# Moving the contents of twelve matmul operand buffers by 4 to 56 elements within their SBUF rows, in a four-layer decoder trunk in float32

## The chip, the cores and the metric

One core of one Trainium2 chip runs the whole program in a single launch. The metric is the device time of one execution in microseconds (us); the kernel before was run three times, and the median is used. "ns" is nanoseconds.

## The reference, cut to what matters

The input x has 512 tokens of 1024 channels. Four blocks follow one another, each added to the residual x: an even mixer (attention with forget gates beside a pooling mixer), a gated MLP, a Conformer convolution module, and a second gated MLP. Nearly all of the arithmetic is in products of a float32 weight matrix with the normed residual or with a hidden array:

```python
def even_mixer(h, ...):                     # h: (512, 1024)
    z = h @ w_in                            # 1024 -> 2056: q, k, v, forget logits, u
    a_out = forgetting_attention(q, k, v, f_logit, q_g, k_g)
    p_out = multiscale_pool(u, w_pool, pool_scale)
    return concat([a_out, p_out]) @ w_out   # 1024 -> 1024
def conformer_conv(h, ...):
    a, g = split(h @ w_pw1, 2)              # 1024 -> 2048
    u = causal_dwconv(a * sigmoid(g), dw_w, dw_b)     # 31 taps
    return silu(layer_norm(u, ln_g, ln_b)) @ w_pw2    # 1024 -> 1024
def conv_ffn(h, ...):                       # twice
    u = causal_dwconv(h @ w_up, conv_w, conv_b)       # 1024 -> 5632, 3 taps
    gate, val = split(u, 2)
    return (silu(gate) * val) @ w_down      # 2816 -> 1024
```

## The kernel before

**Layout.** Channels lie on the 128 partitions and tokens along a partition's row, so an array of 1024 channels is a tile of 8 slices (k = 0 to 7) of 128 x 512. A block of weights is 128 x 1024 (8 slices of 128 x 128), and one block gives one 128-channel slice of an output.

**Three products for one.** Each operand is kept as two tiles of the matmul type `fp32r`: a high part (`wh`, `xh`, `ah`, `mh`, `zh`) and the rest (`wl`, `xl`, `al`, `ml`, `zl`). `products` (L155) issues for every slice three matmuls with 512 columns: stationary `wh` against the moving high part (L159), stationary `wh` against the moving low part (L160), stationary `wl` against the moving high part (L161). One block of weights against 8 slices is therefore 24 matmuls. TensorE loads the stationary operand of a matmul while the one before it runs.

**Weights.** A block comes by DMA from SyncE's queue into `raw` (`load_raw`, L132). ScalarE copies it to `wh` (`w_high`, L137; the copy is L139) and VectorE, or GpSimd in part of the attention, subtracts to make `wl` (`w_low`, L142; L144). Each of the three has three buffers, under one tag `wr`, `wh`, `wl` of the pool `wp`.

**Moving operands.** `Normed` (L189) holds the residual times the norm's weight as `xh` and `xl`, 8 slices each, in one place for the whole kernel. The attention and pooling outputs go to `mh` and `ml` (L341, L342); the MLP's hidden array goes to `ah` and `al`, 22 slices each (L894, L895); the Conformer's to `zh` and `zl`.

**Stages in order.** The attention stage multiplies `xh`/`xl` by 3 + 2 + 8 weight blocks (keys, queries, gate, pooling input), forms the values with `xh`/`xl` as the stationary side, and runs the softmaxes between the products; TensorE's order there is written by hand, and VectorE's and ScalarE's order there is found by a scheduler. Then the output projection (`mh`/`ml`, 8 blocks), the first MLP (up: 44 blocks against `xh`/`xl`; down: 8 outputs of 22 slices against `ah`/`al`), the Conformer stage (16 blocks against `xh`/`xl`, with the taps on VectorE, GpSimd, ScalarE and TensorE in an order that a planner sets, then 8 blocks against `zh`/`zl`), and the second MLP.

**Where the tiles lie.** SBUF addresses are bytes within a partition's row. The program places `xh` at 36,768 and `xl` at 53,152, `wh` at 85,920, 90,016 and 94,112, `wl` at 98,208, 102,304 and 106,400: all seven and more leave 160 modulo 256. `zh` and `zl` also leave 160. `ah` (114,720) and `al` (159,776) leave 32, `mh` (135,392) and `ml` (151,776) leave 224. Slices are 2048 bytes apart in the moving tiles and 512 bytes apart in the weights, so every slice of a tile has its tile's residue.

Of the kernel before, what the change touches and what calls it, by code (L numbers as in the profile page):

```python
# [16 lines left out]
P = 128  # L17
# [18 lines left out]
# Columns of the parameter array, one value per partition and column.  # L36
# [11 lines left out]


class Plan:  # L50
    """Tasks, each on one engine, that are issued in the order of a simulated run: of the tasks
    that can start first, the one with the lowest key does. A task may take slots (of a pool's
    tag, say) that others give back. Costs and lags are in microseconds."""
# [43 lines left out]
def hybrid_trunk(ctx: ExitStack, tc: tile.TileContext, x, prm, w_qk, w_v, w_f, w_u, w_pool,  # L97
# [9 lines left out]
    # PSUM: 8 banks, by use in the attention; the other phases take them in turn  # L107
# [29 lines left out]
    def w_high(raw, shape):  # L137
        wh = wp.tile([P, *shape], F32R, tag="wh", name="wh", bufs=3)
        S.activation(out=wh, in_=raw, func=AF.Copy)  # L139
        return wh  # L140

    def w_low(raw, wh, shape, on=V):  # L142
        wl = wp.tile([P, *shape], F32R, tag="wl", name="wl", bufs=3)
        on.tensor_tensor(out=wl, in0=raw, in1=wh.bitcast(F32), op=ALU.subtract)  # L144
        return wl
# [5 lines left out]
    def load(src, shape, on=V):  # L151
        """A block of weights, and its parts: h + l is the block exactly."""
        return load_parts(load_raw(src, shape), shape, on)

    def products(acc, terms, first=True, last=True):  # L155
        """acc += sum of a.T @ b over (ah, al, bh, bl), each operand in two parts."""
# [6 lines left out]
    def split(src, h, l, g=None):  # L163
        """h + l = src, or src * g with one g per partition."""
# [8 lines left out]
    # A row of T values that all partitions of a 32-partition block hold is folded to T / 32  # L173
    # columns (value 32 j + p at partition p of the block, column j) and unfolded.
# [14 lines left out]
    class Normed:  # L189
        """The residual's parts times the norm's weight, and 1 / rms of every token, which  # L190
        the products are multiplied by afterwards."""

        def __init__(self, gname, goff, tmp):
            self.g, self.goff, self.tmp = gname, goff, tmp
            self.h = per.tile([P, KT, T], F32R, tag="xh", name="xh")
            self.l = per.tile([P, KT, T], F32R, tag="xl", name="xl")
# [31 lines left out]
    def even_layer(next_norm):  # L228
        with tc.tile_pool(name="att", bufs=1) as at, tc.tile_pool(name="att2", bufs=2) as a2, \
                tc.tile_pool(name="att4", bufs=4) as a4:  # L230
            # the first tiles of x and of the weights together, so that the products start early
# [27 lines left out]
            # eps * mean square, for the norms of q and k; 1 / rms with tokens on partitions  # L259
# [25 lines left out]
            # The logits of a head: [qh; qh].T @ [kh; kl] + [ql; row sums].T @ [kh; columns],  # L285
            # where the rows past q and k give c[q] - c[k]. Head 0 of a pair has them below,
            # head 1 above.
# [3 lines left out]
            # log forget gates, their running sum: at partitions 0-31 and 64-95, four times each  # L291
# [32 lines left out]
            # values, tokens on partitions  # L324
            # (where x was: it is loaded again for the residual)
# [15 lines left out]
            mh = at.tile([P, KT, T], F32R, name="mh")  # L341
            ml = at.tile([P, KT, T], F32R, name="ml")  # L342
# [11 lines left out]
            def qk_finish(pr, acc_k, acc_q, m_k, m_q):  # L354
                """The RMS norms of q and k, on products that are not multiplied by 1 / rms
                of x: that only weighs eps. Then the operands of the logits."""
# [70 lines left out]
            # What TensorE does while the softmaxes run: the next pairs' projections, the pooling,  # L427
            # the first outputs' products.
# [8 lines left out]
            def fill():  # L437
# [3 lines left out]
                later = [(1, finish1)]          # (steps to go, what then, a part every step)  # L441
# [577 lines left out]
```

## Time and profile before

| what | value |
|---|---|
| three runs | 1133.15, 1135.85, 1138.61 us (median 1135.85) |
| span of the profiled execution | 1134.6 us |
| its own time beside the median | 1.3 us below it |
| instructions in its trace | 12,732 |
| TensorE matmuls in the trace | 4,876, busy 1093.5 us (96% of the span) |
| VectorE / ScalarE / GpSimd busy | 749.2 / 508.0 / 152.3 us |
| read from HBM | 107.18 MB, 98 GB/s with what is written |

The profile is of one execution. "PE" is TensorE's matmuls and "PEld" its loads of the stationary operand, "DVE" is VectorE, "ACT" ScalarE, "POOL" GpSimd. A matmul's recorded duration reaches past the start of the next one, since matmuls are pipelined, so the cost of a matmul in a dense run is the time from one start to the next, called its spacing below. "L159" is line 159 of the kernel before. A granted clock of 1.00 is TensorE's upper level, 2.4 GHz, and 0.50 its lower one, 1.2 GHz.

### The profile page before, as it was taken

What the parts mean: (1) busy time and instruction counts of PE and PEld (TensorE: products, weight loads), DVE (VectorE), ACT (ScalarE), POOL (GpSimd) and SP (SyncE); (2) the same over time, 40 slices, a digit from 0 to 9 for tenths busy, and PEclk for the clock granted to TensorE, in tenths of its full rate; (3) what the DMA queues carried; (4) which work ended last, traced back from release to release, by engine and by line L of the source; (5) the groups of instructions that cost most, each with busy time, mean ns of one, the idle gap of its engine ahead of it and who ended that gap; (6) DMA issues with size and microseconds to landing.
All of it is one profiled execution on the core that took longest, in us unless ns stands there. A gap on an engine that the chain in (4) does not pass through costs nothing.

```text
span 1134.6 us, 12732 instructions
## 1 busy us (share of the span) xinstructions
PE 1093.5 (96%) x4876; PEld 872.2 (77%) x4876; DVE 749.2 (66%) x1049; ACT 508.0 (45%) x707; POOL 152.3 (13%) x131
## 2 busy tenths in 40 slices
PE   7999989999999999999999997799999999999998
PEld 5778867888888888888877762588888888888886
DVE  5888985677777776333359998777777777752221
ACT  6577644444444444222247544555444444431120
POOL 0031350000000000000039886000000000000000
PEclk9999999999999999999999998899999999999999
DMA  6211024223322233232324535132322232223330
GB/s 229 80 59 38 24 77 167 94 93 101 104 93 93 94 105 94 84 101 85 107 98 134 161 93 142 56 124 98 94 93 93 97 108 93 93 84 120 105 118 19
DMA packets 36972, 111.94 MB, mean 99 GB/s; under 512 B 4144, under 2 KB 4784, under 8 KB 36912
## 3 DMA queue, kind: packets, MB, share of 16 engines
q1 hardware_dynamic: 36912, 111.14, 31.2%
q8 instruction: 38, 0.62, 0.2%
q14 instruction: 22, 0.18, 0.0%
HBM read 107.18 MB, written 3.94 MB: 98 GB/s over the span
## 4 chain that ended last, share of the span: by engine, by line
PE 81%; DVE 8%; ACT 4%; POOL 3%; issue 1%; DMA 1%; POOLq 0%; SPq 0%; ACTq 0%; DVEq 0%
PE bank L161 26%; PE bank L159 26%; PE bank L160 26%; POOL y L733 2%; DVE bank L749 1%; ACT tap L730 1%; ACT wh L139 1%; PE bank L703 1%; DVE u L675 1%; DVE wl L144 1%; PE bank L873 1%; PE bank L874 1%; DMA raw<-in_w_qk 1%; DVE nm L500 1%; DVE pl L167 0%
## 5 line engine op out<-in xcount | busy, mean ns | idle before, releaser
L159 PE MATMUL bank<-xh,wh 128*128 128x512 f32 x936 | 371.3, 397 | 7.0 <-ACT wh L139 6.7
L160 PE MATMUL bank<-xl,wh 128*128 128x512 f32 x936 | 367.7, 393 | 0.0
L161 PE MATMUL bank<-xh,wl 128*128 128x512 f32 x936 | 367.3, 392 | 0.0
L139 ACT ACTIVATE wh<-raw 128x1024 fp32r<-128x1024 f32 (+2 forms) x189 | 193.4, 1026 | 288.3 <-PE bank L160 244.5
L144 DVE TENSOR_TENSOR wl<-raw,wh 128x1024 fp32r<-128x1024 f32 (+2 forms) x178 | 216.6, 1219 | 152.5 <-ACT wh L139 150.5
L159 PEld LDWEIGHTS bank<-xh,wh 128*128 128x128 f32 x936 | 177.3, 190 | 47.3 <-ACT wh L139 7.6
L161 PEld LDWEIGHTS bank<-xh,wl 128*128 128x128 f32 x936 | 177.1, 189 | 38.6 <-DVE wl L144 0.8
L160 PEld LDWEIGHTS bank<-xl,wh 128*128 128x128 f32 x936 | 177.4, 190 | 38.0 <-issue 1.4
L161 PE MATMUL bank<-ah,wl 128*128 128x512 f32 x352 | 139.0, 395 | 0.0
L159 PE MATMUL bank<-ah,wh 128*128 128x512 f32 x352 | 139.0, 395 | 0.0
L160 PE MATMUL bank<-al,wh 128*128 128x512 f32 x352 | 139.0, 395 | 0.0
L910 DVE SCALAR_TENSOR_TENSOR y<-u,pt,y 128x511 f32<-128x511 f32 (+1 forms) x176 | 131.7, 748 | 7.7 <-ACT y L907 4.6
L905 DVE TENSOR_TENSOR u<-bank,rstd 128x512 f32<-128x512 f32 x88 | 60.6, 688 | 79.0 <-PE bank L161 79.0
L733 POOL TENSOR_TENSOR y<-y,tap 128x512 f32<-128x512 f32 x54 | 81.4, 1508 | 10.0 <-ACT tap L730 6.5
L166 ACT ACTIVATE ah<-y 128x512 fp32r<-128x512 f32 x44 | 27.8, 632 | 114.9 <-DVE y L915 114.9
L161 PEld LDWEIGHTS bank<-ah,wl 128*128 128x128 f32 x352 | 66.1, 188 | 16.1
L160 PEld LDWEIGHTS bank<-al,wh 128*128 128x128 f32 x352 | 66.1, 188 | 16.1
L159 PEld LDWEIGHTS bank<-ah,wh 128*128 128x128 f32 x352 | 66.1, 188 | 16.0
L907 ACT ACTIVATE y<-u,pt 128x512 f32<-128x512 f32 x88 | 71.4, 811 | 4.8 <-DVE u L905 3.8
L914 ACT ACTIVATE y<-y 128x512 f32<-128x512 f32 x44 | 27.9, 634 | 83.0 <-DVE y L910 83.0
L219 DVE TENSOR_TENSOR xr<-bank,xr 128x512 f32<-128x512 f32 x32 | 22.0, 691 | 64.0 <-PE bank L161 64.0
L749 DVE SCALAR_TENSOR_TENSOR bank<-u,pt,bank 128x512 f32<-128x512 f32 x79 | 56.7, 747 | 0.7
(190 smaller groups left out, 1050.4 us busy)
## 6 DMA issues: line engine op xcount, KB each, us to landing
raw<-in_w_up SPq DMA_DIRECT2D x88, 512.0 KB, 3.3
raw<-in_w_down SPq DMA_DIRECT2D x32, 512.0 KB, 3.5
raw<-in_w_pw SPq DMA_DIRECT2D x24, 512.0 KB, 3.3
stack<-d SPq DMA_DIRECT2D x28, 256.0 KB, 5.1
raw<-in_w_down SPq DMA_DIRECT2D x16, 384.0 KB, 3.2
xr<-in_x SPq DMA_DIRECT2D x16, 256.0 KB, 6.0
raw<-in_w_qk SPq DMA_DIRECT2D x8, 512.0 KB, 3.3
raw<-in_w_out SPq DMA_DIRECT2D x8, 512.0 KB, 3.3
```

The lines of the kernel that those rows point to most:

```text
L139: S.activation(out=wh, in_=raw, func=AF.Copy)
L144: on.tensor_tensor(out=wl, in0=raw, in1=wh.bitcast(F32), op=ALU.subtract)
L159: PE.matmul(acc, lhsT=ah, rhs=bh, start=(first and i == 0), stop=False)
L160: PE.matmul(acc, lhsT=ah, rhs=bl, start=False, stop=False)
L161: PE.matmul(acc, lhsT=al, rhs=bh, start=False, stop=(last and i == n - 1))
L166: S.activation(out=h, in_=src, func=AF.Copy)
L733: G.tensor_tensor(out=mine["y2"], in0=mine["y2"], in1=mine[s], op=ALU.add)
L749: V.scalar_tensor_tensor(out=acc, in0=shifted(s), scalar=wcol(s), in1=acc, op0=ALU.mult, op1=ALU.add)
L905: V.tensor_tensor(out=u, in0=acc, in1=nrm.r, op=ALU.mult)
L907: S.activation(out=y, in_=u, func=AF.Identity, scale=col("cv_w", 3 * ct + 2), bias=col("cv_b", ct))
L910: V.scalar_tensor_tensor(out=y[:, s:], in0=u[:, 0:T - s], scalar=col("cv_w", 3 * ct + 2 - s), in1=y[:, s:], op0=ALU.mult, op1=ALU.add)
L914: S.activation(out=ys[0], in_=ys[0], func=AF.Silu)
```

## The change

Twelve buffers (three `wh`, three `wl`, and `xh`, `xl`, `ah`, `al`, `mh`, `ml`) are allocated 64 elements longer, and what they hold begins some elements into them. The rotation over three weight buffers, which the pool did under one tag, is now written as three tags taken in turn. No instruction is added or removed on any engine's list of work. Comments are also gone from the file; they are left out here.

```diff
+OFFSETS = {"wh0": 24, "wh1": 28, "wh2": 32, "wl0": 24, "wl1": 28, "wl2": 32,
+           "xh": 24, "xl": 36, "ah": 16, "al": 28, "mh": 56, "ml": 4}
...
+    turns = {"wh": itertools.cycle(range(3)), "wl": itertools.cycle(range(3))}
+
+    def placed(pool, shape, tag, name):
+        n = math.prod(shape)
+        t = pool.tile([P, max(n, 1024) + 64], F32R, tag=tag, name=name, bufs=1)
+        o = OFFSETS[tag]
+        t = t[:, o:o + n]
+        if len(shape) == 1:
+            return t
+        names = "abc"[:len(shape)]
+        return t.rearrange(f"p ({' '.join(names)}) -> p {' '.join(names)}",
+                           **dict(zip(names, shape)))
...
     def w_high(raw, shape):
-        wh = wp.tile([P, *shape], F32R, tag="wh", name="wh", bufs=3)
+        wh = placed(wp, shape, f"wh{next(turns['wh'])}", "wh")
...
     def w_low(raw, wh, shape, on=V):
-        wl = wp.tile([P, *shape], F32R, tag="wl", name="wl", bufs=3)
+        wl = placed(wp, shape, f"wl{next(turns['wl'])}", "wl")
...
-            self.h = per.tile([P, KT, T], F32R, tag="xh", name="xh")
-            self.l = per.tile([P, KT, T], F32R, tag="xl", name="xl")
+            self.h = placed(per, [KT, T], "xh", "xh")
+            self.l = placed(per, [KT, T], "xl", "xl")
...
-            mh = at.tile([P, KT, T], F32R, name="mh")
-            ml = at.tile([P, KT, T], F32R, name="ml")
+            mh = placed(at, [KT, T], "mh", "mh")
+            ml = placed(at, [KT, T], "ml", "ml")
...
-            ah = fp.tile([P, FT, T], F32R, name="ah")
-            al = fp.tile([P, FT, T], F32R, name="al")
+            ah = placed(fp, [FT, T], "ah", "ah")
+            al = placed(fp, [FT, T], "al", "al")
```

An element has 4 bytes. With the allocations that the changed program gets, the contents leave these residues modulo 256 (before in brackets): first weight buffer 0, second 16, third 32, the same for `wh` and `wl` (160); `xh` 0 and `xl` 48 (160); `ah` 96 and `al` 144 (32); `mh` 192 and `ml` 240 (224). `zh`, `zl` and all other tiles keep theirs.

The scheduler, which sees other buffers, also puts some instructions of VectorE and ScalarE in another order between the end of the attention and the start of the output projection; on GpSimd and SyncE the order is the same, and TensorE's differs only in how the three matmuls of neighbouring slices of the output projection follow one another. Here is VectorE's queue before, at the last pooling group: `us` are GpSimd's running sums, `mx` what VectorE makes of them, `nm` and `z` a softmax's row maximum and row sum, `p` its weights, `ml` the low part of a pooling output.

```order
L504 RECIPROCAL z<-z 128x1
L505 TENSOR_SCALAR p<-p,z 128x512
L504 RECIPROCAL z<-z 128x1
L505 TENSOR_SCALAR p<-p,z 128x384
L144 TENSOR_TENSOR wl<-raw,wh 128x128
L170 SCALAR_TENSOR_TENSOR ml<-bank,pt,mh 128x512
L500 TENSOR_REDUCE nm<-bank 128x1
L406 SCALAR_TENSOR_TENSOR mx<-us,u 128x512
L504 RECIPROCAL z<-z 128x1
L408 TENSOR_TENSOR mx<-us,pt 128x15
L505 TENSOR_SCALAR p<-p,z 128x256
```

And the same place in the changed program, where line numbers are 17 higher (L423 was L406, L522 was L505):

```order
L521 RECIPROCAL z<-z 128x1
L522 TENSOR_SCALAR p<-p,z 128x512
L517 TENSOR_REDUCE nm<-bank 128x1
L184 TENSOR_TENSOR pl<-bank,ph 128x128
L423 SCALAR_TENSOR_TENSOR mx<-us,u 128x512
L521 RECIPROCAL z<-z 128x1
L161 TENSOR_TENSOR wl<-raw,wh 128x128
L522 TENSOR_SCALAR p<-p,z 128x384
L187 SCALAR_TENSOR_TENSOR ml<-bank,pt,mh 128x512
L517 TENSOR_REDUCE nm<-bank 128x1
L425 TENSOR_TENSOR mx<-us,pt 128x15
L427 TENSOR_TENSOR mx<-mx,u 128x15
```

The instruction that reads GpSimd's `us` now stands ahead of the scaling of the softmax's 384-column block, the small `wl`, the `ml` and a row maximum, which it followed before.

## Rows read from the trace of the kernel before

**Rows 1.** The profile's page: busy time by engine, and TensorE's clock in 40 slices.
```profile
PE 1093.5 (96%) x4876; PEld 872.2 (77%) x4876; DVE 749.2 (66%) x1049; ACT 508.0 (45%) x707; POOL 152.3 (13%) x131
...
PEclk9999999999999999999999998899999999999999
```

**Rows 2.** The page: the chain that ended last, by engine.
```profile
PE 81%; DVE 8%; ACT 4%; POOL 3%; issue 1%; DMA 1%; POOLq 0%; SPq 0%; ACTq 0%; DVEq 0%
```

**Rows 3.** Waits: who, for whom, us in total, times, longest.
```profile
ACT wh L139 <- PE bank L160: 244.5, 142, 4.8
...
PE bank L159 <- ACT wh L139: 7.0, 2, 6.7
```

**Rows 4.** Windows: stretch, its us; each engine's busy us (instructions); clock, DMA, GB/s.
```profile
240.00:420.00 180.00, 180.00 (x796) 149.05 (x795) 131.71 (x166) 81.88 (x100) 0.00 (x0) 1.00 0.29 97
785.00:985.00 200.00, 200.00 (x884) 165.62 (x883) 146.62 (x185) 90.58 (x112) 0.00 (x0) 1.00 0.30 97
1010.00:1125.00 115.00, 115.00 (x495) 92.51 (x494) 30.28 (x31) 21.40 (x22) 0.00 (x0) 1.00 0.31 95
187.00:212.00 25.00, 25.00 (x111) 20.52 (x110) 18.24 (x24) 11.90 (x17) 0.00 (x0) 1.00 0.42 136
626.90:629.20 2.30, 2.30 (x7) 1.81 (x6) 1.94 (x4) 1.87 (x3) 2.14 (x3) 0.50 1.05 230
600.00:700.00 100.00, 89.51 (x440) 61.71 (x442) 95.99 (x120) 52.15 (x77) 88.97 (x66) 0.94 0.52 133
```

**Rows 5.** Groups of TensorE's instructions by shape: count, busy us, mean ns, idle before.
```profile
L159 PE MATMUL bank<-xh,wh 128*128 128x512 f32 x936 | 371.3, 397 | 7.0 <-ACT wh L139 6.7 <-ACT xh L169 0.3
...
L159 PE MATMUL bank<-ah,wh 128*128 128x512 f32 x352 | 139.0, 395 | 0.0
```

**Rows 6.** Timeline of TensorE in the first MLP's down projection: start us, us, what.
```profile
520.13 0.39 PE L159 MATMUL bank<-ah,wh 128*128 128x512 f32 x1
520.36 0.40 PE L160 MATMUL bank<-al,wh 128*128 128x512 f32 x1
520.60 0.39 PE L161 MATMUL bank<-ah,wl 128*128 128x512 f32 x1
```

**Rows 7.** Timeline of TensorE, 512-column weighted sums of the attention, second head.
```profile
95.44 0.39 PE L160 MATMUL bank<-pl,vhl 128*128 128x512 f32 x1
95.66 0.40 PE L161 MATMUL bank<-ph,vhl 128*128 128x512 f32 x1
95.90 0.34 PE L159 MATMUL bank<-ph,vhl 128*128 128x384 f32 x1
```

**Rows 8.** Timeline of TensorE at the lower clock, Conformer stage.
```profile
626.81 0.63 PE L159 MATMUL bank<-xh,wh 128*128 128x512 f32 x1
...
628.94 0.63 PE L161 MATMUL bank<-xh,wl 128*128 128x512 f32 x1
```

**Rows 9.** Timeline of TensorE after an idle stretch, values stage: first and tenth of a run.
```profile
28.89 0.39 PE L160 MATMUL bank<-wl,xh 128*128 128x512 f32 x1
...
30.97 0.39 PE L160 MATMUL bank<-wl,xh 128*128 128x512 f32 x1
```

**Rows 10.** Timeline of VectorE at the last pooling group; brackets: idle before, releaser.
```profile
160.62 1.00 DVE L505 TENSOR_SCALAR p<-p,z 128x384 f32<-128x384 f32 x1
...
163.26 0.41 DVE L500 TENSOR_REDUCE nm<-bank 128x1 f32<-128x256 f32 x1
165.09 0.69 DVE L406 SCALAR_TENSOR_TENSOR mx<-us,u 128x512 f32<-128x512 f32 x1 [1.42 <-POOL us L401]
```

**Rows 11.** Timeline of TensorE there: three blocks of transposes, and the last weighted sum.
```profile
166.34 0.51 PE L513 MATMUL bank<-ident,p 128*128 128x128 f32 x3
...
168.78 0.38 PE L513 MATMUL bank<-ident,p 128*128 128x128 f32 x2
...
170.39 0.27 PE L513 MATMUL bank<-ident,p 128*128 128x128 f32 x1
...
171.03 0.49 PE L159 MATMUL bank<-ph,vhl 128*128 128x512 f32 x1 [0.37 <-ACT ph L166]
```

## The prediction

> **What bounds the kernel now.** I read the page first. TensorE is busy 96% of the span and at the upper clock in all but a few slices [rows 1], and it holds 81% of the chain that ended last [rows 2]. The list of waits says the same from the other side: ScalarE waits 244.5 us in 142 places for TensorE to give back a `wh` buffer, while TensorE waits 7.0 us for ScalarE's copies [rows 3]. So in the MLPs and the projections weights are ready early, and a matmul's spacing is what counts. The exception is the Conformer stage: between 600 and 700 us VectorE is busy for 95.99 of 100 us [rows 4], so the 16 x 24 = 384 matmuls against `xh`/`xl` there can grow or shrink behind it.
>
> Next I worked out spacings. A window of dense matmuls counts those that hang over its edges, 1.7 of them (a record of 0.39 us over a spacing of 0.23). In the up projections that gives 180 / (796 - 1.7) and 200 / (884 - 1.7), both 226.7 ns; in the second down projection 115 / (495 - 1.7) = 233.1 ns; in the output projection 25 / (111 - 1.7) = 228.7 ns [rows 4]. All have 512 columns, the same types, the same clock of 1.00. At the lower clock, five spacings of the same form take 2.13 us, 426 ns each [rows 4, 8]; that is 512 columns at 1.2 GHz, one per cycle and nothing more. Half of it, 213 ns, would be the same at 2.4 GHz. **So 13 to 20 ns of each spacing at the upper clock are something else.**
>
> What differs between the stages is where the tiles lie. Call d the moving tile's residue less that of the stationary tile being loaded meanwhile, modulo 256. The up projections have d = 0, the output projection 224 - 160 = 64, the down projection 32 - 160, that is 128. The attention's weighted sums, 96 - 160, have 192: two spacings take 0.46 us, 230 ns each, read to 0.01 us [rows 7]. VectorE's load does not explain it: it is busy 73% of the time in the up projection, 26% in the slower down projection [rows 4].
>
> **The change part by part.** It adds no instruction. The three tags in turn repeat what one tag with three buffers did; I cost that at nothing, since the weights' side has the 244.5 us of slack above [rows 3], and a late `wh` would show first there. ScalarE and VectorE now write at 16-byte offsets; the traces show no such row, and the same slack covers it in the projections.
>
> *Spacing.* The new d differ by weight buffer (residues 0, 16, 32) and by tile. I interpolate linearly between the rows, with 226.7 at 0, 228.7 at 64, 233.1 at 128, and 232 at 192 (between the 230 just read and the 233 at 128). Nothing in this trace lies between the multiples of 64, so this is an estimate.
> - `xh` then has d = 0, 240, 224: mean 228.0, +1.3 ns. `xl` has 48, 32, 16: 227.7, +1.0. Two of three spacings move `xh`, so +1.2. The page of groups has 936 x 3 = 2808 of these [rows 5]; less the Conformer's 384 that is 2424, **+2.9 us**.
> - `ah` has 96, 80, 64: 229.8, -3.3 ns; `al` has 144, 128, 112: 232.6, -0.5. Mean -2.4, times 352 x 3 = 1056 [rows 5]: **-2.5 us**.
> - The output projection's 8 x 24 = 192: `mh` 192, 176, 160 gives 232.3, `ml` 229.3, mean +2.6: **+0.5 us**.
> - The Conformer's second product, 192 more: `zh` and `zl` stay, the weights move, so d = 160, 144, 128 in place of 0: 232.8, +6.1 ns, **+1.2 us**.
> - The 96 matmuls of the values stage, +0.1 us.
>
> Together +2.2 us. Taking the trace's rows as the ends, every spacing of the first and fourth item at 226.7 or at 233.1 would give -2 to +17 us; the floor of 213 ns lies far below, and I keep it for a rival. I take +2.2, since these d lie closest to the rows used.
>
> The Trainium skill's page "TensorE: Matmul & The Clock Gate" (section "Back-to-back issue gap") gives N / 2.4 + 2.5 ns, 215.8 ns for 512 columns, at the upper clock. By it the spacing that could be won is 11 to 17 ns and not 13 to 20; the trace shows no dense float32 run at that value.
>
> *Order.* At the last pooling group VectorE waited 1.42 us for GpSimd's `us` and began `mx` at 165.09 us [rows 10]. Before that wait it had done the scaling of the 384-column block (160.62, 1.00 us) and the row maximum of the next block (163.26) [rows 10]. In the changed order both stand behind the wait, with a small `wl` and the `ml`. So the scaled block comes at about 165.1 + 0.7 + 1 + 1 = 167.8 instead of 161.6, and TensorE, which transposes it at 166.34 [rows 11], stands there some 1.5 us. The row maximum moves from 163.3 to 168.5; exponential, scaling and two more blocks follow it, so the last transposes, at 170.39 [rows 11], come about 3 us later, and the weighted sum at 171.03, which waited 0.37 us already, with them. Another block's `wl` ahead of the last pooling `ml` adds a little, and one fewer wait after it gives some back. I take **+3.3 us**, with ends 0 (fill work slides into the gap) and +5 (all of 160 to 165 lost). What is late next is the end of the attention, and all after it.
>
> Sum: 1134.6 + 2.2 + 3.3 = 1140.1 for the profiled execution. It lay 1.3 us under the median of the three runs, so **1141.4 us**, 0.5% above 1135.85. A measurement of this kernel can tell about 0.5%, 5.7 us, from no change; the forecast stands on that edge.
>
> **The rivals.**
> *The residues free the moving stream (faster).* What costs 13 to 20 ns is the load of the next weights taking reads from the moving operand, and some pairs of residues keep them apart. For: the cost is there only at the upper clock, and differs by d [rows 4, 8]. Against: d = 0, which the change mostly leaves or surrounds, is the cheapest of four values seen. If half the way to 213 ns were won, about 2712 matmuls now at 226.7 would give 6.7 ns each (18 us), 1056 would give 10 (10.5 us) and 192 would give 8 (1.5 us): 30 less, 3.3 for the order, 1109 us; all the way, 1079. It decides from 2.3 ns per matmul on: 3960 of them then pay for the order and for 5.7 us.
> *The steady run is lost (slower).* In the up projection every spacing is 226.7. After an idle stretch it is not: the first nine take 2.08 us, 231.1 each [rows 9], and the down projection's run long and short in turn, 0.23 and 0.24 us [rows 6]. So the phase between the two streams matters, and equal residues let it settle at the best. With three weight buffers and two tiles at different residues it might never settle: 2712 x 4.4 = 11.9 us more, the down projections 2.1 less, +0.5 for the rest, +3.3: 1149.5 us. At 238, the largest spacing that a down row allows, it would be above 1165.
> *Residues do nothing, only the order counts.* The spacing would follow from something else that differs by stage, and 1139 us (1136 without the order) comes out. Against it: same shape, same clock, same engine, 6.4 ns apart [rows 4]. The Trainium skill's page "SBUF — State Buffer" (section "Who interferes with whom") speaks for this rival and against the change: TensorE has two independent read ports, one for each operand, and never waits on anyone. By that rule the residue term is zero and 1139 is the time; the trace disagrees in so far as it has the 6.4 ns.
>
> **How the numbers follow.** The forecast has 0.42 (its own range 1133 to 1149: the order's 0 to 5 and some 6 either way for the interpolation), split evenly, 0.22 within 0.5% and 0.20 slower. Freed streams have 0.30, all faster; the lost steady run 0.17, slower; no effect 0.11, within 0.5%. So faster 0.30, same 0.33, slower 0.37. The range runs from 1108, which leaves out the better part of the freed streams (0.12), to 1153, which leaves out the worse part of the lost run (0.06). The forecast's own 1133 to 1149 is the one to look at if the mechanism is as I read it.
>
> **What would show it.** Dense windows of the two up projections: 227 to 229 ns if right, below 222 for the first rival, above 230 for the second, 226.7 unchanged for the third. In the down projections about 231 instead of 233.1; in the Conformer's second product about 233. At the last pooling group a wait of TensorE for VectorE's `p` before the 384-column transposes, and the attention ending about 3 us later. The forecast is wrong if spacings at residues that are not multiples of 64 apart fall outside 226 to 234 ns.

## The result, and the profile after

| kernel | median, us | runs | span of the profiled execution, us |
|---|---|---|---|
| before | 1136.09 | 4 (1133.15 to 1138.61) | 1134.6 |
| changed | 1150.11 | 4 (1148.78 to 1152.01) | 1147.0 |

The changed kernel takes 1.0131 times as long, with a 95% interval of 1.0115 to 1.0148: 14.0 us more, where 5.3 us more was forecast. The time lies inside the range, and the sign is the one that had the largest chance, but the size is that of the second rival (1149.5 us), not of the forecast. The two spans, which the traces can take apart, differ by 12.4 us.

The page of the changed kernel shows nothing else that moved: TensorE is busy 12.2 us longer with the same 4,876 matmuls, its clock has the same pattern, and its share of the chain is larger by two points [rows 1, 2].

```profile
PE 1105.7 (96%) x4876; PEld 870.7 (76%) x4876; DVE 751.7 (66%) x1049; ACT 504.2 (44%) x707; POOL 152.2 (13%) x131
...
PEclk9999999999999999999999998899999999999999
...
PE 83%; DVE 7%; ACT 4%; POOL 4%; issue 2%; DMA 1%; POOLq 0%; SPq 0%; ACTq 0%; DVEq 0%
...
L176 PE MATMUL bank<-xh,wh 128*128 128x512 f32 x936 | 375.3, 402 | 7.5 <-ACT wh L156 7.5
...
L176 PE MATMUL bank<-ah,wh 128*128 128x512 f32 x352 | 138.5, 393 | 0.0
```

In the groups by shape (the last two lines; L176 was L159) a matmul on `xh` reads 402 ns where it was 397, and one on `ah` 393 where it was 395 [rows 5]. These durations reach into the next matmul, so the spacing comes from dense windows, as before: time over the count less 1.7. The windows of the changed kernel are the output projection, the two up projections and the two down projections (stretch, its us; busy us and instructions of each engine; clock, DMA, GB/s):

```profile
187.00:212.00 25.00, 25.00 (x110) 20.21 (x109) 15.84 (x20) 11.01 (x15) 0.00 (x0) 1.00 0.33 106
240.00:420.00 180.00, 180.00 (x776) 145.31 (x775) 129.24 (x163) 77.29 (x96) 0.00 (x0) 1.00 0.29 95
790.00:990.00 200.00, 200.00 (x862) 161.45 (x861) 144.29 (x182) 86.85 (x108) 0.00 (x0) 1.00 0.29 95
1025.00:1140.00 115.00, 115.00 (x498) 93.12 (x497) 29.16 (x29) 20.88 (x22) 0.00 (x0) 1.00 0.30 92
470.00:570.00 100.00, 100.00 (x433) 80.99 (x432) 34.81 (x39) 28.45 (x34) 0.00 (x0) 1.00 0.32 97
```

180 / (776 - 1.7) and 200 / (862 - 1.7) are both 232.5 ns, against 226.7 in the same stages before [rows 4]. Down it is 100 / (433 - 1.7) = 231.9 and 115 / (498 - 1.7) = 231.7 ns, against 233.1. In the output projection's 25 us one matmul more or less in 110 is 2 ns, so there the spacing is better read from start to start: between 187 and 212 us it is 232.4 against 228.9. The two up projections have 2 x 44 x 24 = 2112 matmuls, so **5.8 ns x 2112 = 12.2 us** more; the down projections give back 1.3 x 1056 = 1.4 us; the output projection adds 3.5 x 192 = 0.7 us. From the first to the last matmul each up projection is longer by 6.05 us, each down projection shorter by 0.8 (1.6 together) and the output projection longer by 0.7, and the Conformer stage between the MLPs is 1.1 us longer. The clock is 1.00 in every one of these windows, in both kernels, and no instruction waits in them: the same matmuls start further apart.

The place at the last pooling group, on which the order term rested, looks as follows in the changed kernel (VectorE, then TensorE; start us, us, what, and in brackets the idle time before it and who ended it):

```profile
163.86 0.69 DVE L423 SCALAR_TENSOR_TENSOR mx<-us,u 128x512 f32<-128x512 f32 x1 [3.10 <-POOL us L418]
...
164.54 0.27 DVE L161 TENSOR_TENSOR wl<-raw,wh 128x128 fp32r<-128x128 f32 x1
164.73 0.41 DVE L522 TENSOR_SCALAR p<-p,z 128x384 f32<-128x384 f32 x1
```

```profile
154.60 0.40 PE L530 MATMUL bank<-ident,p 128*128 128x128 f32 x2
...
156.61 0.50 PE L176 MATMUL bank<-mh,wh 128*128 128x512 f32 x1 [0.91 <-ACT wh L156]
...
159.04 0.51 PE L178 MATMUL bank<-mh,wl 128*128 128x512 f32 x1 [1.71 <-POOL wl L161]
...
164.20 0.63 PE L530 MATMUL bank<-ident,p 128*128 128x128 f32 x4
...
166.34 0.52 PE L530 MATMUL bank<-ident,p 128*128 128x128 f32 x3
...
171.19 0.50 PE L176 MATMUL bank<-ph,vhl 128*128 128x512 f32 x1 [0.37 <-ACT ph L183]
```

VectorE does stand 3.10 us before `mx`, as forecast, where it stood 1.42 before [rows 10]. But the scaling of the 384-column block behind it is done at 165.14, and TensorE transposes that block at 166.34 without a wait, as before [rows 11]. The scaling takes 0.41 us there, where it took 1.00 [rows 10]. What is new stands some ten microseconds before those transposes: TensorE waits 0.91 us for ScalarE's `wh`, and 1.71 us for GpSimd's `wl`, in the first block of the output projection. In the kernel before that stretch has one wait:

```profile
155.75 0.44 PE L513 MATMUL bank<-ident,p 128*128 128x128 f32 x2
...
160.28 0.50 PE L161 MATMUL bank<-mh,wl 128*128 128x512 f32 x1 [1.72 <-POOL wl L144]
...
164.21 0.63 PE L513 MATMUL bank<-ident,p 128*128 128x128 f32 x4
```

From the two transposes to the group of four it took 8.46 us before and 9.60 after. The changed kernel was 1.2 us ahead here (its first transposes of this kind start at 67.83 us, those of before at 69.05), so the lost 1.1 us doesn't show in the time of day at 164.2.

### The profile page after: what moved, and what is told of

It reads as the page before. It is cut to its first block, busy times and chain, and to the rows that moved or that the text cites. A ratio compares the mean times of both kernels' runs of the same rounds, so it can differ in the third digit from the quotient of the medians.

```text
span 1147.0 us, 12729 instructions
## 1 busy us (share of the span) xinstructions
PE 1105.7 (96%) x4876; PEld 870.7 (76%) x4876; DVE 751.7 (66%) x1049; ACT 504.2 (44%) x707; POOL 152.2 (13%) x131
## 4 chain that ended last, share of the span: by engine, by line
PE 83%; DVE 7%; ACT 4%; POOL 4%; issue 2%; DMA 1%; POOLq 0%; SPq 0%; ACTq 0%; DVEq 0%
PE bank L176 26%; PE bank L178 26%; PE bank L177 26%; POOL y L750 3%; DVE bank L766 1%; PE bank L720 1%; ACT tap L747 1%; ACT wh L156 1%; DVE u L692 1%; DVE wl L161 1%; PE bank L890 1%; PE bank L891 1%; PE bank L530 0%; POOL wl L161 0%; DMA raw<-in_w_f 0%
## 5 line engine op out<-in xcount | busy, mean ns | idle before, releaser
L176 PE MATMUL bank<-xh,wh 128*128 128x512 f32 x936 | 375.3, 402 | 7.5 <-ACT wh L156 7.5
L178 PE MATMUL bank<-xh,wl 128*128 128x512 f32 x936 | 371.3, 397 | 0.0
L156 ACT ACTIVATE wh<-raw 128x1024 fp32r<-128x1024 f32 (+2 forms) x189 | 193.1, 1024 | 299.7 <-PE bank L177 258.9
L161 DVE TENSOR_TENSOR wl<-raw,wh 128x1024 fp32r<-128x1024 f32 (+2 forms) x178 | 215.8, 1214 | 155.2 <-ACT wh L156 153.5
L176 PEld LDWEIGHTS bank<-xh,wh 128*128 128x128 f32 x936 | 177.0, 189 | 52.2 <-ACT wh L156 8.4
L176 PE MATMUL bank<-ah,wh 128*128 128x512 f32 x352 | 138.5, 393 | 0.0
L176 PEld LDWEIGHTS bank<-ah,wh 128*128 128x128 f32 x352 | 66.0, 188 | 15.2
```

Of the source, the lines that this page charges most:

```text
L176: PE.matmul(acc, lhsT=ah, rhs=bh, start=(first and i == 0), stop=False)
L178: PE.matmul(acc, lhsT=al, rhs=bh, start=False, stop=(last and i == n - 1))
```

## The experiments

Fifteen kernels ran. Residues are modulo 256; d is the prediction's difference, moving less loaded tile. Each diff is against the changed kernel unless it says otherwise. A mean over a window is time over the count less 1.7, as before; single spacings are read from start to start. Where only one execution was made, it stands beside the median of the kernel before on the same chip (1133.37 us for experiments 1 to 4, 1134.46 for 5, 6, 10 and 11, 1134.86 for 7 to 9 and 12, 1135.25 for 13 to 15).

### 1. All tiles at one residue

```diff
-OFFSETS = {"wh0": 24, "wh1": 28, "wh2": 32, "wl0": 24, "wl1": 28, "wl2": 32,
-           "xh": 24, "xl": 36, "ah": 16, "al": 28, "mh": 56, "ml": 4}
+OFFSETS = {"wh0": 0, "wh1": 0, "wh2": 0, "wl0": 0, "wl1": 0, "wl2": 0, "xh": 0,
+           "xl": 0, "ah": 32, "al": 32, "mh": 48, "ml": 48, "zh": 0, "zl": 0}
...
-            zh = cv.tile([P, KT, T], F32R, name="zh")
+            zh = placed(cv, [KT, T], "zh", "zh")
...
-            zl = cv.tile([P, KT, T], F32R, tag="zl", name="zl")
+            zl = placed(cv, [KT, T], "zl", "zl")
```

> All twelve tiles and zh, zl at residue 160, so that moving and loaded tile never differ (d = 0) in any stage. Theory A (only the difference counts, and equal residues settle in a steady run): up projections 226.7 ns as before the change, down projections fall from 233.1 to 226.7 (1056 x 6.4 ns = 6.8 us), output projection from 228.7 to 226.7 (0.4 us), so about 1129 us. Theory B (the down projection is slower for another reason than its residue): down projections stay at 233.1 and the time is that of the kernel before, 1136 us.

1130.72 us against 1133.37, a ratio of 0.9972 (0.9961 to 0.9982). A window in the second down projection:

```profile
1010.00:1115.00 105.00, 105.00 (x465) 87.02 (x464) 27.89 (x28) 19.73 (x20) 0.00 (x0) 1.00 0.33 101
```

105 / (465 - 1.7) = 226.6 ns: with equal residues the down projection runs like the up projection, 6.5 ns below what it took at d = 128. That the down projections are slow by nature is refuted.

### 2. The same, at another place

All tiles at 0 in place of 160 (`w` and `x` 24, `a` 56, `m` 8, `z` 24).

> The same with all at residue 0, so that only the absolute place is another. Theory A (only the difference counts): 226.7 ns in all dense stages and the same time as with 160, within 3 us. Theory C (a start on a multiple of 64 or 256 bytes saves reads): spacings below 224 ns and at least 10 us less.

1131.11 us, one execution, and the dense stages again at 226.7 ns. The place itself does not count.

### 3. Only the weight buffers apart

```diff
-           "xh": 24, "xl": 36, "ah": 16, "al": 28, "mh": 56, "ml": 4}
+           "xh": 24, "xl": 24, "ah": 16, "al": 28, "mh": 56, "ml": 4}
```

> The change with xh and xl both at 0; the weight buffers stay at 0, 16 and 32, so d is 0, 240 or 224 for a whole block of 24 matmuls and changes from block to block. Theory A1 (what is lost is the steady run, by d changing from matmul to matmul): blocks in the first buffer come back to 227 ns after a few matmuls, the up projections' mean falls from 232.4 to below 230, and each up stage is 2.5 us shorter or more. Theory A2 (each d has its own price and 0 alone is cheap): first buffer 227, the two others stay at 230 or above. Theory D (the price is that of the rotation): no change from 232.4.

1140.75 us, one execution. The window of the first up projection, and from TensorE's timeline the first matmuls of four blocks in turn, whose weights lie at 16, 32, 0 and 16:

```profile
240.00:420.00 180.00, 180.00 (x787) 147.71 (x787) 130.80 (x165) 80.63 (x99) 0.00 (x0) 1.00 0.29 97
```

```profile
242.09 0.39 PE L176 MATMUL bank<-xh,wh 128*128 128x512 f32 x1
...
247.54 0.39 PE L176 MATMUL bank<-xh,wh 128*128 128x512 f32 x1
...
253.14 0.39 PE L176 MATMUL bank<-xh,wh 128*128 128x512 f32 x1
...
258.58 0.39 PE L176 MATMUL bank<-xh,wh 128*128 128x512 f32 x1
```

The mean is 180 / (787 - 1.7) = 229.2 ns. A block of 24 matmuls takes 5.45 us with weights at 16, 5.60 at 32, 5.44 at 0: 227, 233 and 227 ns. So two buffers run as before, and one does not.

### 4. Only the moving tiles apart

```diff
-OFFSETS = {"wh0": 24, "wh1": 28, "wh2": 32, "wl0": 24, "wl1": 28, "wl2": 32,
+OFFSETS = {"wh0": 24, "wh1": 24, "wh2": 24, "wl0": 24, "wl1": 24, "wl2": 24,
```

> The change with all weight buffers at 0; xh stays at 0 and xl at 48, so d is 0 for two spacings in three and 48 for the third, the same in every block. Theory A1 (changing d breaks the run): the up projections stay near 232. Theory A2 (each d has its own price): the spacings with d = 0 are 227 and only those that move xl are longer, mean 228 to 230. Theory D (the rotation of the weights' residues is what costs): back to 227.

1158.70 us, one execution, the slowest of all.

```profile
240.00:420.00 180.00, 180.00 (x766) 143.35 (x765) 128.70 (x160) 77.12 (x96) 0.00 (x0) 1.00 0.28 93
790.00:990.00 200.00, 200.00 (x851) 159.25 (x850) 142.78 (x178) 86.40 (x109) 0.00 (x0) 1.00 0.29 95
```

235.5 ns in both up projections, 8.8 more than before, though two of three matmuls there have d = 0 and all weights share a residue. Read one by one, the matmuls with d = 0 take 233 to 235 ns, and three spacings repeat: 233, 238, 235. Weights apart alone cost 2.5 ns, moving tiles apart alone 8.8, both together (the change) 5.8: **the parts do not add up**, and a price for each d cannot give these numbers.

### 5. Each product's own pair equal, the pairs apart

```diff
+OFFSETS = {"wh0": 24, "wh1": 24, "wh2": 24, "wl0": 36, "wl1": 36, "wl2": 36,
+           "xh": 24, "xl": 36, "ah": 16, "al": 28, "mh": 56, "ml": 4, "zh": 24, "zl": 36}
```

While `xh`, `xl`, `xh` stream, the loads are of `wh`, `wl`, `wh`; with `wl` and `xl` both at 48 and `wh` and `xh` both at 0, d = 0 for all three. `zh` and `zl` are placed as in the first experiment.

> xh at residue 0 and xl at 48 as in the change, but wh at 0 and wl at 48 in all buffers. The moving tiles differ by 48 as in the run before this one, while every tile is loaded against a moving tile of its own residue, so d = 0 in all three spacings. Theory A (only the difference between the moving and the loaded tile counts): up projections back to 226.7 ns from 235. Theory D (two moving tiles at different residues cost by themselves): near 235. The down projections have d = 96 in all three spacings and show the steady price of that.

1151.77 us, one execution.

```profile
240.00:420.00 180.00, 180.00 (x781) 146.29 (x780) 129.55 (x164) 78.21 (x98) 0.00 (x0) 1.00 0.29 94
790.00:990.00 200.00, 200.00 (x859) 160.88 (x858) 142.70 (x179) 87.00 (x110) 0.00 (x0) 1.00 0.29 95
```

231.0 and 233.3 ns with d = 0 throughout, in two stages that have the same residues. That only the difference to the loaded tile counts is refuted.

### 6. The kernel before, with the down and output operands moved to the weights' residue

Against the kernel before:

```diff
-            mh = at.tile([P, KT, T], F32R, name="mh")
-            ml = at.tile([P, KT, T], F32R, name="ml")
+            mh = at.tile([P, KT * T + 64], F32R, name="mh")
+            ml = at.tile([P, KT * T + 64], F32R, name="ml")
+            mh, ml = [t[:, 48:48 + KT * T].rearrange("p (k t) -> p k t", t=T) for t in (mh, ml)]
...
-            ah = fp.tile([P, FT, T], F32R, name="ah")
-            al = fp.tile([P, FT, T], F32R, name="al")
+            ah = fp.tile([P, FT * T + 64], F32R, name="ah")
+            al = fp.tile([P, FT * T + 64], F32R, name="al")
+            ah, al = [t[:, 32:32 + FT * T].rearrange("p (k t) -> p k t", t=T) for t in (ah, al)]
```

> The kernel before, its pools and its order of instructions untouched, with only ah, al, mh and ml moved to residue 160, so that d = 0 everywhere. Theory A: down projections 226.7 ns in place of 233.1, 1056 x 6.4 = 6.8 us less, output projection 0.4 us less: 0.6% faster than before. If the scheduler's other order costs something in the attention, this run is 1 to 3 us below the one with all tiles at 160 in the changed program's order (0.28% faster than before); if the order costs nothing, both have the same time.

1127.57 us against 1134.46, a ratio of 0.9932 (0.9916 to 0.9948): **6.9 us below the kernel before**, and the fastest form together with the fourteenth experiment's.

```profile
187.00:212.00 25.00, 25.00 (x112) 20.71 (x111) 17.55 (x23) 11.20 (x17) 0.00 (x0) 1.00 0.43 143
240.00:420.00 180.00, 180.00 (x796) 149.05 (x795) 131.18 (x165) 81.46 (x100) 0.00 (x0) 1.00 0.30 97
...
1010.00:1115.00 105.00, 105.00 (x465) 86.95 (x464) 27.26 (x27) 19.73 (x20) 0.00 (x0) 1.00 0.32 101
```

All three stages come to 226.6 or 226.7 ns. 6.4 x 1056 = 6.8 us from the down projections and 2.0 x 192 = 0.4 from the output projection make 7.2.

### 7. The change's structure with the old residues

```diff
+OFFSETS = dict.fromkeys(["wh0", "wh1", "wh2", "wl0", "wl1", "wl2",
+                         "xh", "xl", "ah", "al", "mh", "ml"], 0)
```

> The changed program with all twelve offsets at 0: its longer buffers, its three tags and its order of instructions, but every residue as before the change. The two parts of the change come apart here. If the other order costs what the difference between the two runs with d = 0 says (0.9972 and 0.9932 of before), this one is 3 to 5 us slower than before, 1.003 to 1.004, and the residues then cost the remaining 9 to 11 us of the change's 14. If the order is free (TensorE was not late at the place that the prediction named), it equals before within 1.5 us and the residues cost all of it.

1136.97 us against 1134.86, a ratio of 1.0020 (1.0009 to 1.0030): of the 14 us, 2.1 belong to the tags and the order that comes with them, the rest to the residues. The dense stages are those of before; the time goes at the place that the changed kernel's timeline showed. TensorE's timeline here:

```profile
154.71 0.43 PE L530 MATMUL bank<-ident,p 128*128 128x128 f32 x2
...
156.76 0.50 PE L176 MATMUL bank<-mh,wh 128*128 128x512 f32 x1 [0.91 <-ACT wh L156]
...
159.19 0.79 PE L178 MATMUL bank<-mh,wl 128*128 128x512 f32 x1 [1.71 <-POOL wl L161]
...
165.87 0.63 PE L530 MATMUL bank<-ident,p 128*128 128x128 f32 x4
```

11.16 us from the two transposes to the four, against 8.46 before: 2.7 us. And behind the two waits the clock is down, as a window of this trace shows:

```profile
160.70:162.40 1.70, 1.70 (x6) 1.37 (x5) 0.81 (x2) 0.95 (x3) 1.64 (x3) 0.50 0.62 253
```

TensorE had been idle 0.91 and 1.71 us with two matmuls between, and the granted clock in this window is then 0.50, the lower level. The changed kernel, with the same two waits and the clock at 1.00, lost 1.1 us here, so some 1.6 of the 2.7 us are the clock's. After the single wait of 1.72 us before, and after the same two waits in the changed kernel, the records show 1.00.

The cause of the wait for `wh`, which the kernel before does not have, is in the buffers. The rows on the order ahead of the prediction carry no buffer numbers, and read without them ScalarE's and GpSimd's queues are alike there. With them, the first two blocks of the output projection (1561, which TensorE uses first, and 1591) change places on both, and so do two blocks just ahead of them. ScalarE's list before, then in the changed program (place in the list, line, what):

```
149 L139 ACTIVATE wh_1561<-raw_1559 128x1024
159 L139 ACTIVATE wh_1591<-raw_1589 128x1024
```

```
149 L156 ACTIVATE wh_1591<-raw_1589 128x1024
159 L156 ACTIVATE wh_1561<-raw_1559 128x1024
```

Under one tag the pool gave block 1561 the first buffer, which was free, and 1591 the third. The strict turn gives 1561 the third, which TensorE still reads for the last pooling-input block (its last matmul starts at 155.3 us in the changed kernel). So the second block is copied first, and the first one's `wh` and `wl` come late in succession.

### 8. Half the loads in the up projections

Against the kernel before; the second and third matmul of each slice but the last use 64 stationary columns. It leaves out half of the low-order products of the up projections.

```diff
+                    for k in range(KT):
+                        bh, bl = nrm.h[:, k], nrm.l[:, k]
+                        PE.matmul(acc, lhsT=wh[:, k], rhs=bh, start=(k == 0), stop=False)
+                        m = P if k == KT - 1 else P // 2
+                        PE.matmul(acc[0:m], lhsT=wh[:, k, 0:m], rhs=bl, start=False, stop=False)
+                        PE.matmul(acc[0:m], lhsT=wl[:, k, 0:m], rhs=bh, start=False,
+                                  stop=(k == KT - 1))
```

> The kernel before, with the second and third matmul of each slice but the last in the up projections given 64 stationary columns in place of 128; it leaves out half of the low-order products there. It asks what the 13.4 ns over 213.3 are. Theory L (the load of the next stationary tile takes reads from the moving tile): the two spacings in which 64 columns are loaded lose half of the excess, about 220 ns, and the third, which loads 128, stays near 227; mean 222, each up stage 4 to 5 us shorter. Theory F (a fixed cost of every float32 matmul): all stay at 226.7.

1141.09 us, one execution: slower, not faster.

```profile
240.00:420.00 180.00, 180.00 (x786) 122.75 (x785) 130.25 (x165) 80.41 (x99) 0.00 (x0) 1.00 0.29 96
```

The loads are busy 122.75 us of the 180 in place of 149.05 [rows 4], and the spacing rises from 226.7 to 180 / (786 - 1.7) = 229.5 ns. Neither theory had this. It does not settle what the 13 ns over 213 are; it shows that matmuls of 128 and 64 stationary columns in turn also leave the pattern of 226.7 ns, at residues that are all equal.

### 9. The pairs 64 apart

`wl`, `xl`, `ml` and `zl` at 224, all else at 160.

> The run with pairs apart once more, with the low tiles 64 bytes from the high ones and not 48: xh and wh at 160, xl and wl at 224, so d = 0 in all three spacings of the up projections. If 64 bytes, 16 float32 elements, are a unit of the moving stream's reads, the run settles again and the spacing is 226.7; if any two residues do harm, it stays at 231 to 233 as with 48. In the down projections both moving tiles are at 160, so d is 0, 192, 0.

1145.68 us, one execution.

```profile
240.00:420.00 180.00, 180.00 (x781) 146.35 (x780) 129.59 (x164) 78.43 (x98) 0.00 (x0) 1.00 0.29 94
```

231.0 ns: steps of 64 bytes are no better.

### 10 to 12. One d for a whole stage

All weights at 160, `zh` and `zl` placed as in the first experiment, and one residue for the moving tiles of each stage: up 176, down 192, output 208, Conformer 240; then 0, 16, 48, 64; then 152, 168, 96, 112.

> All weights at 160, and one d for each stage: up projections 16, down 32, output projection 48, Conformer's second product 80. With one d throughout a stage, theory A1 (equal d lets the run settle) says that each stage repeats a short pattern of spacings; at 240 and 0 it settled at 226.7, at 224 at 233, at 64 at 228.7, at 128 at 233.1. By nearness d = 16 gives 226.7 (as 240 does) and 32, 48 and 80 lie between 228 and 234. A stage below 226 would show that the equal residue is not the best.

> As the run before this one, with d = 96 in the up projections, 112 in the down projections, 144 in the output projection, 160 in the Conformer's second product. By nearness to 128 all lie between 230 and 235 ns; the up projections then cost 2112 x 4 to 8 ns, 8 to 17 us more than before. A stage below 226 ns would show a better place than equal residues.

> As the two other runs with one d for each stage: up projections 248 (8 bytes back), down 8, output projection 192, Conformer's second product 208. d = 0 and 240 settle at 226.7, 16 does not. If the steady run needs the moving tile at the same 16-byte line as the loaded one or at one behind, 248 settles at 226.7 and 8 does not; if it needs the exact residue, neither does; if a step inside 16 bytes is harmless, both do. 192 and 208 by nearness 231 to 234.

1149.24, 1151.91 and 1150.80 us, one execution each. The first up projections of the three:

```profile
240.00:420.00 180.00, 180.00 (x779) 146.10 (x778) 128.58 (x162) 78.72 (x98) 0.00 (x0) 1.00 0.29 94
```

```profile
240.00:420.00 180.00, 180.00 (x773) 144.79 (x772) 128.57 (x161) 77.94 (x97) 0.00 (x0) 1.00 0.28 94
```

```profile
240.00:420.00 180.00, 180.00 (x778) 146.45 (x776) 129.09 (x163) 78.19 (x98) 0.00 (x0) 1.00 0.29 94
```

That is 231.6, 233.4 and 231.9 ns for d = 16, 96 and 248. With the other stages and kernels, d for a whole stage gives, from start to start:

| d | 0 | 8 | 16 | 32 | 48 | 64 | 80 | 96 | 112 | 128 | 144 | 160 | 192 | 208 | 248 |
|---|---|---|---|---|---|---|---|---|---|---|---|---|---|---|---|
| ns | 226.7 | 233.3 | 231.7 | 233.3 | 233.3 | 228.9 | 231.1 | 233.3 | 231.1 | 233.3 | 233.3 | 234.3 | 233.3 | 234.7 | 232.0 |

There is one low value in this table, at 0, with 64 next; all else lies between 231 and 235 with no slope that a line between neighbours would follow. None comes near the 213 ns of the first rival.

### 13 and 14. The buffers in the old sequence

```diff
-    turns = {"wh": itertools.cycle(range(3)), "wl": itertools.cycle(range(3))}
+    places = [0, 1, 2] * 5 + [0, 2, 1, 0, 2, 0, 1, 2, 2] + [0, 1, 2] * 55
+    turns = {"wh": iter(places), "wl": iter(places)}
```

Once with the old residues (7), once with all at 160 (1). With this sequence every engine's instructions stand in the order of the kernel before.

> The kernel of the seventh experiment (longer buffers, three tags, all contents at the old residues), but the nine weight blocks from the sixteenth to the twenty-fourth take the three tags in the sequence in which the pool of the kernel before gave out its buffers; every engine's instructions then stand in the order of the kernel before. Theory T (the strict turn puts the first block of the output projection into the buffer of the last pooling-input block, which TensorE still reads, so ScalarE and GpSimd serve the second block first and TensorE waits for the first one's wh and wl in succession): the 0.91 us wait of TensorE for ScalarE's wh goes, the time from the two transposes near 155 us to the four near 165 us falls from 11.2 to 8.4 us as in the kernel before, and the time equals the kernel before within 0.1% (1.002 before). Rival U (the tags or the longer buffers themselves cost, or something elsewhere): the ratio stays near 1.002, about 2.3 us.

> The first experiment (all tiles at residue 160) with the same sequence of tags. Theory T: 11 to 8.4 us in the same place, and the time of the sixth experiment, a ratio of about 0.993. Rival U: the first experiment's ratio of 0.997.

1134.65 us against 1135.25, a ratio of 0.9994 (0.9985 to 1.0003), where the strict turn gave 1.0020; and 1127.47, a ratio of 0.9932 (0.9920 to 0.9944), where it gave 0.9972. TensorE in the first of the two:

```profile
155.23 0.43 PE L531 MATMUL bank<-ident,p 128*128 128x128 f32 x2
...
159.76 0.50 PE L179 MATMUL bank<-mh,wl 128*128 128x512 f32 x1 [1.71 <-POOL wl L162]
...
163.68 0.62 PE L531 MATMUL bank<-ident,p 128*128 128x128 f32 x4
```

8.45 us, and the wait for `wh` is gone. Longer buffers and tags cost nothing; the strict turn, with the order that comes with it, cost it all.

### 15. Nearly equal residues

All weights at 160; up at 144, down at 152, output at 164, Conformer at 156.

> All weights at residue 160, moving tiles at one residue per stage: up projections d = 240, down projections 248, output projection 4, second Conformer product 252. If what settles is a moving residue 0 or 16 bytes below the weights', the up projections run at 226.7 ns like the one weight buffer of the third experiment, and the time of the up projections is that of the kernel before; if a settled run needs all residues equal, they come out at 231 to 234 ns and that buffer was an effect of its neighbours. Down at 248: 232 if the value of the up projections at 248 is a property of d, else anything from 226.7 to 234. Output at 4 and Conformer at 252 show whether a single element off equality is enough to lose the run: then 231 to 234, else 226.7.

1152.71 us, one execution.

```profile
187.00:212.00 25.00, 25.00 (x106) 19.88 (x106) 14.72 (x19) 11.02 (x15) 0.00 (x0) 1.00 0.32 106
240.00:420.00 180.00, 180.00 (x773) 144.76 (x773) 128.73 (x161) 77.55 (x97) 0.00 (x0) 1.00 0.29 94
790.00:990.00 200.00, 200.00 (x847) 160.99 (x846) 142.55 (x178) 84.91 (x106) 0.00 (x0) 1.00 0.28 94
```

The two up projections have the same residues, yet one takes 233.4 ns and the other 200 / (847 - 1.7) = 236.6. The output projection, a single element above, takes 237.9 ns from start to start in its window, the largest mean of all; down at 248 it is 231.4. The Conformer's second product, a single element below (252), does both. After a pause at 745.4 us its mean is 230.4, but the 54 spacings between these two starts take 12.24 us, 226.7 ns each:

```profile
731.76 0.39 PE L891 MATMUL bank<-zh,wl 128*128 128x512 f32 x1
...
744.00 0.39 PE L891 MATMUL bank<-zh,wl 128*128 128x512 f32 x1
```

So an unequal residue does not always lose the 226.7 ns. The buffer at 16 in the third experiment, with the same d of 240 as the up projections here, kept it from the block before it; d alone does not give it. That the run's history decides is the likely reading, and no run tests it.

Read one by one, the spacings show more: at unequal residues a dense run settles too, at another pattern. The first up projection here repeats 233, 233, 234 ns and the second 234, 239; with all residues equal it is 226, 227, 227. In the changed kernel each block falls within ten matmuls into the pattern of its buffer (233, 238, 235 in the buffer at 0, as in the fourth experiment), and the blocks take 5.52, 5.60 and 5.62 us in turn, each round of three the same 16.74 us:

```profile
242.95 0.40 PE L176 MATMUL bank<-xh,wh 128*128 128x512 f32 x1
...
259.69 0.40 PE L176 MATMUL bank<-xh,wh 128*128 128x512 f32 x1
...
276.43 0.40 PE L176 MATMUL bank<-xh,wh 128*128 128x512 f32 x1
```

## Why the prediction was wrong, point by point

**What bounds it: right.** All of the change is in spacings of dense matmuls and in one place of the attention; ScalarE's and VectorE's copies at 16-byte offsets cost nothing that shows (`wh` 1024 ns against 1026, `wl` 1214 against 1219).

**The spacing term failed at its first step, a price for each d.** The prediction set 226.7 at d = 0 and drew lines to 64, 128 and 192, +1.2 ns for an up matmul. Measured are +5.8: 12.2 us for the up projections alone, where it had 2.9 for these and the attention together. Grouped by tile, the changed kernel itself has the up matmuls at d = 0 at 233.3 ns, the value that was to be 226.7. The values that the lines went through held within 1.3 ns (d = 192 came out at 233.3, not 232); what they stood for did not. The fourth and fifth experiments show that the spacing goes with the residues of all tiles of a run together, not with d pair by pair; the fifth and fifteenth, that the same residues can run in two patterns of different means. One residue for both moving and both loaded tiles gave 226.7 ns in every dense stage, and nothing else tried did for a whole stage. So the term forecast at +2.2 us measured about +12.3 in the stages outside the attention (from first to last matmul 12.1 in the up projections, -1.6 in the down projections, 0.7 in the output projection, and 1.1 in the Conformer stage). Its ends by the trace's rows add up to -2 and +15 us, not +17.

**Down, output, Conformer: the sign right.** -1.3 ns down where -2.4 was forecast (1.4 to 1.6 us given back, not 2.5), +0.7 us in the output projection where +0.5, and 1.1 us more in the Conformer stage where 1.2. Since the price for each d is wrong, that the last two come near is luck.

**"The three tags in turn cost nothing" failed.** It was argued from ScalarE's 244.5 us of slack [rows 3], some 209 of which lie in the MLPs and only 14 in the attention. There a buffer by strict turn can be one that is still read, and "a late `wh` would show first there" is what happened: 1.1 us in the profiled execution, 2.1 us by the seventh experiment's runs.

**The order term, +3.3 us, failed at the time of the scaled block.** VectorE's wait grew as forecast, but the block was done at 165.14 us, not at 167.8, 1.2 us before its transposes. GpSimd's `us` came 1.2 us earlier, and behind it the small `wl` and the scaling took 0.27 and 0.41 us, where the forecast had 1 each from rows in which GpSimd was still summing. So none of the 1.5 or 3 us came; the weighted sum starts at 171.19, against 171.03 before. What was lost near there came with the strict turn of the tags.

**The rivals.** The second one came nearest: what is lost is the pattern of 226.7 ns. It put the rest at 231.1 ns; it is 232.5, and that the run "might never settle" did not come true: the changed kernel settles in every block, at a dearer pattern. That its 1149.5 us lies so near is partly luck: 3.3 of it was the order. The first, a moving stream that comes free, has nothing for it in the fifteen values of d. The third, that residues do nothing, is refuted by the first and sixth experiments. Runs here also speak against the rule of the Trainium skill's page "SBUF — State Buffer" (section "Who interferes with whom") that stood beside it, that TensorE's two read ports are independent and it never waits: as the prediction read it, the seventh kernel and the changed one, with the same instructions in the same order, would take the same time, and they differ by 1.1%. Whether the ports are where it is lost, no run shows. The 215.8 ns of the Trainium skill's page "TensorE: Matmul & The Clock Gate" (section "Back-to-back issue gap") was reached as a mean by no dense stage here; 226.7 is the best. The section gives that figure for a matmul by itself, and a lower one for a stream with weight loads, which the prediction passed over.

**What stays open.** Why equal residues settle at the shortest pattern and others at longer ones, what chooses between two patterns of the same residues, and what the 13 ns are that remain (at the upper level, 2.4 GHz, 226.7 ns are 544 periods, 32 more than the columns). The eighth experiment was to show whether they are the load; it left the pattern and so told nothing of it. Nor is it known why the clock fell behind the two waits in the seventh kernel and not in the changed one.

## What to carry to other kernels

A property seen in four stages that differ in one number is not yet a function of that number: before interpolating, ask whether the low value is a point or the bottom of a slope, and give the case that it is a point its full price. For dense float32 products made of high and low parts, put every tile that TensorE reads, moving and stationary, at one residue modulo 256 bytes; here that gained 0.7% by four padded buffers. And when a pool's rotation is written out by hand, compare which buffer each block gets, with its numbers, not only the order of the instructions.

## What was not expected of the hardware

- One element (4 bytes) between moving and loaded tiles can be enough to lose the 226.7 ns: 237.9 in the output projection with the moving tile above; with it below, in the Conformer, 226.7 held for 54 spacings and 230.4 followed.
- The same residues in two stages with the same instructions gave 233.4 and 236.6 ns (231.0 and 233.3 in the fifth experiment), each in a pattern that repeats: at unequal residues a run settles too, and not always at the same value.
- Shorter loads in two of three matmuls made the dense run slower, 229.5 against 226.7 ns.
- The absolute place does not count: all at 0 and all at 160 gave the same 226.7 ns.
